# Two halves of a weighted sum made one task in a planned attention kernel

## The chip, the cores and the metric

One core of a Trainium2 chip runs the kernel. The metric is the time of one execution on the device in microseconds (us). The engines are called by their short names where rows are quoted: PE is TensorE (PEld its weight loads), DVE is VectorE, ACT is ScalarE, POOL is GpSimd, SP issues most DMAs.

## The reference

A backbone of two layers works on 512 latent tokens and 256 context tokens of width 1024. Each layer mixes tokens with three groups of heads that read one projection, joins their normalised outputs through one output projection, and then applies a SwiGLU feed-forward block. Two of the groups are attentions, and the change lies in them:

```python
# A: 6 heads of neighbourhood attention; a latent token sees a 2-D window and all context tokens
p = jax.nn.softmax(s.astype(jnp.float32), axis=-1).astype(v.dtype)
out = jnp.einsum('bhqrc,brqchd->bqhd', p_loc, v_win) + jnp.einsum('bhql,blhd->bqhd', p_ctx, v_ctx)
# C: 6 query heads over 2 key heads, all latent and context keys
s = jnp.einsum('bqkgd,bskd->bkgqs', q, k) * scale
p = jax.nn.softmax(s.astype(jnp.float32), axis=-1).astype(v.dtype)
return jnp.einsum('bkgqs,bskd->bqkgd', p, v)
```

Context tokens attend to context alone, and only in the first layer, since the output holds latent tokens only.

## The kernel before, in words

The attention of a layer is cut into units: one head and one tile of 128 queries. A latent unit of group A has 4 chunks of 128 keys, one of group C has 6, a context unit has 2. Layer 0 has 36 units of each group, layer 1 has 24 of each (no context queries). A unit goes through these steps: `scores` (L1311, TensorE, into a bank of the ring of PSUM tiles; 5 or 6 of them with group A, 3 wide ones with group C), `row_min` (VectorE, L1323 or L1329), `exps` (ScalarE, L1335), `trans` (L1343, TensorE transposes the probabilities chunk by chunk in place), `copy_p` (ScalarE L344 or VectorE L1349, from the bank into the tile `pT`; the bank is then free).

Two units in a row make a pair. `pv` (L1365) forms their weighted sums: for each chunk one matmul of the values with the transposed probabilities for each of the two units, whose results go to the lower and the upper 64 partitions of one of two PSUM banks called `aux`. Then come `evac` (L1371, VectorE copies the sum into `oT`), `back` (L1376, TensorE transposes it into another part of the same bank) and `norm` (L1381, two VectorE instructions that scale the rows by the reciprocal sums; the bank `aux` is free after them). The two `aux` banks also serve the transposes of other steps: `half` (L1408) for the operands of group C and `turn` (L1502) for the merged outputs of the groups, which the output projection then reads (`mtmp`, `xh`, `xl`). The last tile's outputs are turned by a step of the following phase (L1811). Matmuls of the projections go through one helper (L702 to L704).

The order of the instructions is set by a planner (`Plan`, L186 to L235). Each step is a task with an engine, an estimated duration, a priority, the tasks that it depends on, and tokens that it takes and gives (banks, tiles). The planner goes through an estimated time, and whenever an engine is free it emits the task with the lowest priority value that may start. A task is emitted whole, and the order in which tasks are emitted is the order in each engine's queue. At L1480 and L1481 `pv` is two tasks of one half of the chunks each. Both depend on the copies of both units, the first takes the bank, the second gives the two `pT` tiles back, and other TensorE tasks of lower priority value may be emitted between them. The projection weights of the next phase are split into two parts by ScalarE and VectorE or GpSimd, into tiles whose memory the attention's scratch tiles held before.

## Time and profile before

| | |
|---|---|
| median of 3 runs | 1722.39 us (1721.97 to 1726.96) |
| profiled execution, by its span | 1724.7 us |
| instructions | 25956 |
| TensorE busy | 1640.9 us, 95% |
| VectorE busy | 1085.3 us, 63% |
| ScalarE busy | 570.8 us, 33% |
| GpSimd busy | 940.8 us, 55% |

The profile gives no other time of the profiled execution than its span, from the first to the last instruction. The attention phase of layer 0 lies between some 205 and 372 us, that of layer 1 between some 1185 and 1304 us. A row of stretches names a window of time, its length, and the busy time of PE, PEld, DVE, ACT and POOL with the number of instructions, then the granted clock of TensorE as a share of the full one, the busy share of the DMA engines and GB/s. A row of waits names who waited for whom, the total in us, how often, and the longest. A row of the timeline has the start, the time until the last instruction of the group ended, the engine, line and operation; matmuls are pipelined, so that their rows overlap, and the step from one start to the next tells what one costs. The trace has two records for each matmul of the weighted sums.

### The profile page before, as it was taken

The numbers are of one execution on the slowest core, as the hardware profiler recorded it, in microseconds if no ns is written. First come the engines' busy times: TensorE is split into PE (matmuls) and PEld (weight loads), VectorE is DVE, ScalarE is ACT, GpSimd is POOL, SyncE is SP. The second block draws the span as 40 slices with busy tenths as digits, with TensorE's granted clock in tenths as the row PEclk, the third lists the DMA queues.
The fourth block names the chain that finished last, engine by engine and source line by source line (L and its number), as shares of the span: only waits on it lengthen the run. The fifth ranks groups of instructions, "written<-read, shape, count | busy, mean of one in ns | idle before, by whom it ended". The sixth has DMA issues, their size and how long they took to land. (4 is left out here: it accounts for less than half of the span.)

```text
span 1724.7 us, 25956 instructions
## 1 busy us (share of the span) xinstructions
PE 1640.9 (95%) x10438; PEld 1411.3 (82%) x10438; DVE 1085.3 (63%) x1691; ACT 570.8 (33%) x995; POOL 940.8 (55%) x683
## 2 busy tenths in 40 slices
PE   7999889999899999999999998998999999999997
PEld 5998767899888787887778878986889888888886
DVE  7567778748678796887932288527856544433435
ACT  5322368735411111111111234226764422222211
POOL 1764574434536664666744448445434466765762
PEclk9999999999999999999999999999999999999999
DMA  9326353041244423334231122212104133222211
GB/s 350 90 84 207 115 190 115 2 160 32 97 146 142 139 98 128 123 115 142 98 123 52 70 83 88 74 57 75 39 25 171 50 136 121 98 98 98 98 50 49
DMA packets 40264, 182.41 MB, mean 106 GB/s; under 512 B 4480, under 2 KB 6400, under 8 KB 29136
## 3 DMA queue, kind: packets, MB, share of 16 engines
q1 hardware_dynamic: 38336, 176.75, 29.3%
q0 software_dynamic: 1664, 3.75, 0.9%
q8 instruction: 82, 1.34, 0.3%
q14 instruction: 38, 0.31, 0.1%
q10 hardware_dynamic: 144, 0.26, 0.0%
HBM read 176.51 MB, written 6.78 MB: 106 GB/s over the span
## 5 line engine op out<-in xcount | busy, mean ns | idle before, releaser
L2005 POOL TENSOR_TENSOR x<-x,ytmp 128x1024 f32<-128x1024 f32 x90 | 249.3, 2793 | 26.7 <-DVE ytmp L2004 26.7
L347 POOL TENSOR_TENSOR gl<-sg,gh 128x512 fp32r<-128x512 f32 (+1 forms) x58 | 96.3, 1661 | 281.6 <-DVE gh L688 281.6
L652 DVE SCALAR_TENSOR_TENSOR msum<-raw,cs,msum 128x1024 f32<-128x1024 f32 x112 | 204.5, 1861 | 21.2 <-DMA raw<-in_w_mod_dram 21.2
L1980 DVE TENSOR_TENSOR sg<-sg,ff_ps 128x512 f32<-128x512 f32 (+1 forms) x58 | 34.4, 593 | 265.1 <-PE ff_ps L704 264.9
L2004 DVE TENSOR_TENSOR ytmp<-y_ps,g 128x512 f32<-128x512 f32 x180 | 119.0, 684 | 51.1 <-PE y_ps L704 51.0
L1979 ACT ACTIVATE sg<-ff_ps 128x512 f32<-128x512 f32 (+1 forms) x58 | 30.3, 523 | 293.6 <-PE ff_ps L704 293.6
L344 ACT ACTIVATE wc<-raw 128x1024 fp32r<-128x1024 f32 x52 | 52.7, 1053 | 160.7 <-PE y_ps L704 140.1
L702 PE MATMUL y_ps<-wc,gh 128*128 128x512 f32 x248 | 98.7, 398 | 0.0
L703 PE MATMUL y_ps<-wc,gh 128*128 128x512 f32 x248 | 98.0, 395 | 0.0
L704 PE MATMUL y_ps<-wc,gl 128*128 128x512 f32 x248 | 97.9, 395 | 0.0
L344 ACT ACTIVATE wa<-raw 128x1024 fp32r<-128x1024 f32 x60 | 62.2, 1056 | 105.0 <-PE ff_ps L703 43.4
L704 PE MATMUL ff_ps<-xh,wb 128*128 128x512 f32 x240 | 93.4, 389 | 0.0
L702 PE MATMUL ff_ps<-xh,wb 128*128 128x512 f32 x240 | 93.4, 389 | 0.0
L703 PE MATMUL ff_ps<-xl,wb 128*128 128x512 f32 x240 | 93.4, 389 | 0.0
L347 POOL TENSOR_TENSOR wb<-raw,wb 128x1024 fp32r<-128x1024 f32 x25 | 65.9, 2636 | 49.1 <-ACT wb L344 48.9
L347 POOL TENSOR_TENSOR wa<-raw,wa 128x1024 fp32r<-128x1024 f32 x29 | 78.0, 2689 | 20.2 <-ACT wa L344 20.1
L702 PE MATMUL ff_ps<-xh,wa 128*128 128x512 f32 x224 | 87.3, 390 | 0.0
L703 PE MATMUL ff_ps<-xl,wa 128*128 128x512 f32 x224 | 87.3, 390 | 0.0
L704 PE MATMUL ff_ps<-xh,wa 128*128 128x512 f32 x224 | 87.2, 389 | 0.0
L344 ACT ACTIVATE wb<-raw 128x1024 fp32r<-128x1024 f32 x54 | 55.4, 1056 | 88.1 <-DMA raw<-in_w_ffn_in_dram 39.8
L347 POOL TENSOR_TENSOR Kl<-kT,Kh 64x768 fp32r<-64x768 f32 x24 | 49.0, 2042 | 64.9 <-ACT Kh L344 61.6
L1343 PE MATMUL ring<-ident,p 128*128 128x128 f32 x528 | 75.1, 279 | 1.9 <-ACT p L1335 1.6
(527 smaller groups left out, 5421.4 us busy)
## 6 DMA issues: line engine op xcount, KB each, us to landing
raw<-in_w_ffn_in_dram SPq DMA_DIRECT2D x44, 1024.0 KB, 5.0
raw<-in_w_mod_dram SPq DMA_DIRECT2D x40, 1024.0 KB, 5.2
raw<-in_w_ffn_out_dram SPq DMA_DIRECT2D x22, 1024.0 KB, 5.0
raw<-in_w_in_dram SPq DMA_DIRECT2D x18, 1024.0 KB, 4.9
wm<-in_w_mod_dram SPq DMA_DIRECT2D x8, 1024.0 KB, 9.8
raw<-in_w_o_dram SPq DMA_DIRECT2D x8, 1024.0 KB, 5.1
tbz<-in_mask_dram SPq DMA_DIRECT2D x12, 384.0 KB, 3.4
x<-in_x_dram SPq DMA_DIRECT2D x8, 512.0 KB, 6.5
```

Of the source, the lines that this page charges most:

```text
L344: nc.scalar.activation(out=o, in_=i, func=AF.Copy, scale=scale)
L347: e.tensor_tensor(out=o, in0=a, in1=b, op=ALU.subtract)
L652: nc.vector.scalar_tensor_tensor(out=o, in0=w[:, i, :], scalar=c, in1=o, op0=ALU.mult, op1=ALU.add)
L702: nc.tensor.matmul(o, lhsT=lh, rhs=rh, start=(i == 0), stop=False)
L703: nc.tensor.matmul(o, lhsT=lh, rhs=rl, start=False, stop=False)
L704: nc.tensor.matmul(o, lhsT=ll, rhs=rh, start=False, stop=(i == n - 1))
L1343: nc.tensor.transpose(un.S[:, c:c + P], un.pt[:, j * P:(j + 1) * P], ident)
L1979: nc.scalar.activation(out=sg, in_=ab[0], func=AF.Silu)
L1980: nc.vector.tensor_tensor(out=sg, in0=sg, in1=ab[1], op=ALU.mult)
L2004: nc.vector.tensor_tensor(out=tmp[:, sl], in0=o, in1=G[1 if t >= NL else 0][:, sl], op=ALU.mult)
L2005: nc.gpsimd.tensor_tensor(out=x[:, t, :], in0=x[:, t, :], in1=tmp, op=ALU.add)
```

## The change

The two tasks of `pv` become one, with twice the estimated duration, the priority of the first half, the dependences of both, and both sets of tokens. The matmuls and their order inside a pair stay. The rest of the diff drops texts in quotes and comments, which moves line numbers by two or three (L1365 becomes L1363, L1376 L1374, L1408 L1406, L1502 L1499, L1811 L1808).

```diff
-        def pv(m, part):
-            """Outputs of two units, transposed, in the two halves of the partitions."""
+        def pv(m):
+
             pair = units[2 * m:2 * m + 2]
             u0 = pair[0]
-            if part == 0:
-                u0.o = aux.pop(0)
-            h = u0.nch // 2
-            for i in range(part * h, part * h + h):
+            u0.o = aux.pop(0)
+            for i in range(u0.nch):
                 for d, un in enumerate(pair):
                     nc.tensor.matmul(u0.o[d * HD:(d + 1) * HD, 0:P], lhsT=un.vs[i], rhs=un.pT[:, i, :], start=(i == 0), stop=(i == u0.nch - 1))
...
             h = {2: 0.27, 4: 0.54, 6: 0.8}[un.nch]
             c0, c1 = cpy_of[i - 1], cpy_of[i]
-            a_ = pn.op(PE, h, call(pv, m, 0), (c0[0], c1[0]), i + 1.7, take=("aux",), kind="pv " + un.kind)
-            b_ = pn.op(PE, h, call(pv, m, 1), (a_, c0[-1], c1[-1]), i + 1.8, give=("pT", "pT"), kind="pv " + un.kind)
+            b_ = pn.op(PE, 2 * h, call(pv, m), (*c0, *c1), i + 1.7, take=("aux",), give=("pT", "pT"), kind="pv " + un.kind)
```

Since the planner's inputs change, its order changes in both attention phases, and with it the order on the other engines. Three places on TensorE follow; a row names the line, the operation, what is written and read, the size and a count.

The first place is in the grouped-query units of layer 1, where the score matmuls of one unit (`ring` from `Kh`, `Kl` and `Q`) stand among the weighted sums. Before:

```order
L1365 MATMUL aux_10623<-pT,vc 64x128 x6
L1311 MATMUL ring_11271<-Kh,Q 128x512
L1311 MATMUL ring_11271<-Kl,Q 128x512
L1311 MATMUL ring_11271<-Kh,Q 128x256
L1311 MATMUL ring_11271<-Kl,Q 128x256
L1365 MATMUL aux_10623<-pT,vc 64x128 x6
L1502 MATMUL aux_10624<-ident,qT 128x128 x4
```

With the change:

```order
L1311 MATMUL ring_11295<-Kh,Q 128x512
L1311 MATMUL ring_11295<-Kl,Q 128x512
L1311 MATMUL ring_11295<-Kh,Q 128x256
L1311 MATMUL ring_11295<-Kl,Q 128x256
L1363 MATMUL aux_10623<-pT,vc 64x128 x12
L1374 MATMUL aux_10624<-ident,oT 128x128
```

The four score matmuls no longer stand between two runs of six; the twelve of a pair are one run. Over both phases the runs of weighted sums between other work number 91 before (56 in layer 0, 35 in layer 1) and 55 now (33 and 22).

The second place is the end of the attention of layer 1: the last weighted sums, the first two blocks of the output projection (24 matmuls each, of which the first rows are shown), and the transposes of the third tile's outputs, `qk`. Before:

```order
L1376 MATMUL aux_10623<-ident,oT 128x128
L1365 MATMUL aux_10624<-pT,vc 64x128 x6
L702 MATMUL ring_11273<-wa,xh 128x256
...
L1376 MATMUL aux_10624<-ident,oT 128x128
L1502 MATMUL aux_10623<-ident,qk 128x128 x3
L702 MATMUL ring_11273<-wa,xh 128x256
```

With the change:

```order
L1363 MATMUL aux_10623<-pT,vc 64x128 x12
L1374 MATMUL aux_10624<-ident,oT 128x128
L702 MATMUL ring_11294<-wa,xh 128x256
...
L1374 MATMUL aux_10623<-ident,oT 128x128
L702 MATMUL ring_11294<-wa,xh 128x256
...
L1499 MATMUL aux_10624<-ident,qk 128x128 x3
L702 MATMUL ring_11293<-wa,xh 128x256
```

The transposes of `qk` stood ahead of the second block and now stand behind it, right ahead of the third. The transposes of the last tile (L1811, now L1808) stood behind the third block, and now stand four blocks of `wb`, `wc` and `cb` later and more.

The third place is in the neighbourhood units of layer 1, around the transposes of the first operands of group C (`qn`). Before:

```order
L1365 MATMUL aux_10624<-pT,va 64x128 x4
L1343 MATMUL ring_10632<-ident,p 128x128 x4
L1343 MATMUL ring_10633<-ident,p 128x128 x4
L1376 MATMUL aux_10624<-ident,oT 128x128
L1408 MATMUL aux_10623<-identr,qn 128x128 x3
L1343 MATMUL ring_10628<-ident,p 128x128 x4
```

With the change:

```order
L1363 MATMUL aux_10624<-pT,va 64x128 x8
L1343 MATMUL ring_10633<-ident,p 128x128 x4
L1343 MATMUL ring_10628<-ident,p 128x128 x4
L1406 MATMUL aux_10623<-identr,qn 128x128 x3
L1374 MATMUL aux_10624<-ident,oT 128x128
L1363 MATMUL aux_10624<-pT,va 64x128 x8
```

A transpose back and the next weighted sum in the same bank now follow each other with nothing between. Layer 0 has one more such place; before there is none.

## The prediction

> **What bounds the kernel now.** I read the profile's head first, then a table of stretches that cuts out both attention phases, then TensorE's own waits in them, and last the timeline of TensorE around the changed matmuls.
>
> ```profile
> span 1724.7 us, 25956 instructions
> PE 1640.9 (95%) x10438; PEld 1411.3 (82%) x10438; DVE 1085.3 (63%) x1691; ACT 570.8 (33%) x995; POOL 940.8 (55%) x683
> ```
>
> TensorE is busy for 1640.9 of 1724.7 us. A change of its own work pays where it is busy without a gap, so the average over the program is not enough. The stretches, with columns for busy time of TensorE, its weight loads, VectorE, ScalarE and GpSimd, then the granted clock and DMA:
>
> ```profile
> 205.40:270.00 64.60, 58.12 (x507) 43.07 (x504) 50.61 (x136) 44.55 (x114) 37.65 (x23) 0.95 0.57 193
> 270.00:350.00 80.00, 79.11 (x742) 65.21 (x736) 59.98 (x148) 61.62 (x147) 37.99 (x53) 1.00 0.11 38
> 350.00:372.00 22.00, 22.00 (x203) 20.85 (x202) 9.57 (x16) 11.06 (x25) 11.35 (x14) 1.00 0.44 164
> 1185.00:1227.00 42.00, 36.57 (x361) 30.70 (x362) 37.99 (x101) 32.16 (x71) 30.01 (x19) 1.00 0.21 69
> 1227.00:1286.00 59.00, 58.35 (x569) 49.45 (x568) 43.47 (x95) 41.59 (x88) 23.18 (x32) 1.00 0.03 10
> 1286.00:1304.50 18.50, 16.65 (x128) 16.45 (x127) 7.05 (x10) 9.66 (x16) 7.26 (x9) 0.91 0.56 196
> ```
>
> The first three rows are layer 0: neighbourhood units, grouped-query units, their end. The last three are the same of layer 1. In the grouped-query stretches TensorE misses 0.9 of 80 us, nothing of 22 and 0.65 of 59 us, with VectorE at 75% and 74%: time taken off TensorE there should come out at the end. In the neighbourhood stretches it misses 6.5 of 64.6 us and 5.4 of 42 us, and in layer 1 VectorE is busy for 38.0 of the 42: there only part of it will pay. TensorE's waits (total, times, longest), layer 0 in the first two rows, layer 1 in the others:
>
> ```profile
> PE aux L1376 <- DVE oT L1371: 3.1, 2, 1.6
> PE aux L1365 <- DVE qT L1381: 2.3, 1, 2.3
> ...
> PE aux L1376 <- DVE oT L1371: 4.2, 3, 2.0
> PE ring L1811 <- POOL qk L1806: 1.9, 1, 1.9
> PE aux L1365 <- DVE qT L1381: 1.0, 1, 1.0
> ```
>
> These rows name the changed matmuls' neighbours: the transpose back (L1376) waits for the evacuation of a weighted sum (7.3 us in all), and a weighted sum (L1365) for a bank that the norms before it have to free (3.3 us).
>
> **The change, part by part.** Removed is the cut of each pair's weighted sum into two tasks. The matmuls stay: the orders of both kernels hold 528 at this line. Both halves already depended on the same two copies, so no half could start earlier than the whole can. What the cut cost is seen in the timeline (start, duration, then the instruction; the trace has two records to each of these matmuls):
>
> ```profile
> 310.34 0.28 PE L1311 MATMUL ring<-Kh,Q 128*128 128x256 f32 x1
> 310.45 0.28 PE L1311 MATMUL ring<-Kl,Q 128*128 128x256 f32 x1
> 310.66 0.44 PE L1365 MATMUL aux<-pT,vc 128*64 128x128 f32 x4
> 311.03 0.39 PE L1311 MATMUL ring<-Kh,Q 128*128 128x256 f32 x1
> 311.25 0.28 PE L1311 MATMUL ring<-Kl,Q 128*128 128x256 f32 x1
> 311.46 1.53 PE L1365 MATMUL aux<-pT,vc 128*64 128x128 f32 x24
> 312.92 0.33 PE L1376 MATMUL aux<-ident,oT 128*128 128x128 f32 x1
> 313.09 0.82 PE L1343 MATMUL ring<-ident,p 128*128 128x128 f32 x6
> 313.74 0.27 PE L1376 MATMUL aux<-ident,oT 128*128 128x128 f32 x1
> 313.85 1.04 PE L1343 MATMUL ring<-ident,p 128*128 128x128 f32 x8
> ...
> 314.94 0.60 PE L1502 MATMUL aux<-ident,qT 128*128 128x128 f32 x4
> 315.30 0.36 PE L1311 MATMUL ring<-Kh,Q 128*128 128x256 f32 x1
> 315.50 0.28 PE L1311 MATMUL ring<-Kl,Q 128*128 128x256 f32 x1
> ```
>
> Read start to start. A score matmul of 256 columns takes 0.11 (310.34 to 310.45) but 0.21 when a weighted sum follows (310.45 to 310.66): entering costs 0.10. Four records take 0.37 (310.66 to 311.03) and 24 take 1.46 (311.46 to 312.92): 1.09/20 = 0.0545 each, hence a fixed 0.37 - 4 x 0.0545 = 0.15 per run of them. The first score behind takes 0.22 in place of 0.11 (311.03 to 311.25): leaving costs 0.11. Leaving towards transposes costs less: the transpose behind the 24 takes 0.17, the next such one 0.11 (313.74 to 313.85), so 0.06. Nothing of this waits for data; no releaser stands at these rows. One run of weighted sums between other work therefore costs 0.10 + 0.15 + 0.06 = 0.31 us between transposes and 0.36 between scores. I take 0.31.
>
> [...]
>
> How often the cut costs it follows from the order: runs of weighted sums between other TensorE work fall from 91 to 55, 36 fewer. By stage: layer 0 neighbourhood 23 to 16, grouped-query 33 to 17; layer 1 14 to 11 and 21 to 11. That is 36 x 0.31 = 11.2 us of TensorE time, 26 x 0.31 = 8.1 of it in the grouped-query stretches that have no gaps, 10 x 0.31 = 3.1 in the neighbourhood stretches.
>
> Against it stand four terms, since the planner now places everything in both phases anew.
>
> Scores behind transposes: 45 such places become 53. The first score behind transposes takes 0.20 (315.30 to 315.50) in place of 0.11, so 8 x 0.09 = 0.7 us.
>
> Neighbourhood stretches: 3.1 us is at stake, and with 6.5 and 5.4 us of gaps present between nothing and all of it pays. I take half: 1.5 lost. The middle is as good as any since VectorE has slack in layer 0 (50.6 of 64.6) and little in layer 1.
>
> New short waits: work of one pair now stands closer to the next step. In two places the order has a transpose back and the next weighted sum in the same bank with nothing between, which no place of before has. There TensorE must wait for the two norms that free the bank:
>
> ```profile
> L1381 DVE TENSOR_SCALAR qT<-aux,rsm x60: 264/275/285, 217.0 to 1229.1; 128x64 f32<-128x64 f32 x60
> ```
>
> 0.27 for the transpose and 2 x 0.24 to 0.28 for the norms, with the handing over some 0.9 us, twice. The other direction exists too: a bank is now taken once and not held while other work runs between two halves, which works on the 3.3 us of bank waits above. From below I allow 3.3 us of gain (all of them vanish), from above 5 us of loss (half of the 10.6 us of waits at L1376 and L1365 once more). I take a loss of 2.0, the two known places and little else.
>
> The end of layer 1's attention. The order shows the transposes of the third tile's outputs (L1502) moved behind the second early block of the output projection. Rows of before, with the last weighted sum first:
>
> ```profile
> 1284.85 0.88 PE L1365 MATMUL aux<-pT,vc 128*64 128x128 f32 x12
> ...
> 1288.75 0.49 PE L1502 MATMUL aux<-ident,qk 128*128 128x128 f32 x3
> 1289.41 0.88 ACT L344 ACTIVATE mtmp<-aux,gout 128x128 f32<-128x128 f32 x3 [3.45 <-PE aux L1502]
> 1290.37 0.83 POOL L1525 TENSOR_TENSOR xh<-mtmp,zero 128x384 fp32r<-128x384 f32 x1 [2.60 <-ACT mtmp L344]
> 1291.28 1.02 POOL L347 TENSOR_TENSOR xl<-mtmp,xh 128x384 fp32r<-128x384 f32 x1
> 1292.33 1.06 ACT L344 ACTIVATE wb<-raw 128x1024 fp32r<-128x1024 f32 x1 [0.52 <-POOL xl L347]
> ...
> 1296.84 0.55 PE L1811 MATMUL ring<-ident,qk 128*128 128x128 f32 x3 [1.85 <-POOL qk L1806]
> ```
>
> From the transposes (1288.75) to the end of `xl` (1292.30) is 3.55 us. Before, an early block of about 2.9 us (24 x 0.12) covers that; now the third block, which needs `xl`, stands right behind, so TensorE waits about 3.55 - 0.45 = 3.1 us. In return the transposes of the last tile (L1811) move behind four more blocks, and their wait of 1.85 goes: 3.1 - 1.85 = 1.3 us lost. Queued behind `xl` are also the two weight copies on ScalarE (`wb`) and their differences on VectorE; the first copy takes 1.06 us by its row, and with a second copy, the square that stands between them and the last difference they need about 3.8 us after it, and the third block with its 2.9 us and the first half of the next cover that. After its gap the trace shows a lower granted clock (the third number from the end of a stretch's row):
>
> ```profile
> 1296.00:1300.00 4.00, 3.16 (x20) 3.16 (x21) 3.97 (x5) 1.62 (x4) 0.79 (x1) 0.76 0.67 231
> 1300.00:1304.00 4.00, 4.00 (x30) 4.00 (x30) 0.06 (x1) 2.01 (x2) 0.70 (x1) 0.81 1.03 385
> ```
>
> 0.76 and 0.81 for 4 us each, 0.24 x 4 + 0.19 x 4 = 1.7 us. If the longer gap doubles that, the loss is 3.0. I take 2.0.
>
> [...]
>
> The end of layer 0's attention has more cover than before (one early block between the last sum and its transpose back, and the blocks behind are in the same order), and no gap today: nothing. Behind both phases the weights stream as they do now.
>
> Sum: 11.2 - 0.7 - 1.5 - 2.0 - 2.0 = 5.0 us. The profiled execution took 1724.7 by its span; the runs go from 1721.97 to 1726.96 with a median of 1722.39, so 1719.7 for the former and **1717.4** for the median.
>
> **The rivals.** *The waits go with the cut.* The fused sum holds banks shorter; the 3.3 us of bank waits go and no new ones come: 11.2 - 0.7 - 1.5 + 3.3 - 1.3 = 11.0, 1711.4. For it: those waits are named. Against: two new tight places.
>
> *TensorE's gain turns into waits.* Three banks circle through scores, minimum, exponential, transposes, copy; when TensorE is faster the circle may become the bound. Then the 8.1 us of the grouped-query stretches go at least half: 5.0 - 4.0 = 1.0, 1721.4. For it: ScalarE and VectorE at 77% and 75% are not far off. Against: 0.9 us of gaps in 80.
>
> *Slower: the long block delays the circle.* Place: the pairs of grouped-query units whose sum has 24 records. Price: the block lasts 1.46 where one half lasted 0.81 (316.84 to 317.65 below), so a transpose or score that becomes ready in it comes up to 0.65 us later.
>
> ```profile
> 316.84 0.88 PE L1365 MATMUL aux<-pT,vc 128*64 128x128 f32 x12 [0.36 <-ACT mtmp L344]
> 317.65 0.44 PE L1343 MATMUL ring<-ident,p 128*128 128x128 f32 x2
> ```
>
> There are 24 such pairs by the order (288 of the 312 grouped-query matmuls, 12 each). If all pay, 24 x 0.65 = 15.6: 1717.4 + 15.6 = 1733. It decides from 16 pairs on (16 x 0.65 = 10.4, past 1727.6). Against: a late engine only costs if TensorE has nothing else to do, and today it always has.
>
> *The change doesn't do what it says:* the 0.3 us is no price of the switch and is paid elsewhere. Then only the losses are left: 1722.4 + 0.7 + 2.0 + 2.0 = 1727.
>
> **How the numbers follow.** My forecast (1713.5 to 1721) has 0.45, the vanishing waits 0.20, the gain turned into waits 0.20, the long block 0.11, the last 0.04. A measurement of this kernel can tell about 0.3%, 5.2 us, from no change: 1717.2 to 1727.6. Half of my forecast's chance lies below that and all of the vanishing waits: faster 0.43. Slower is the long block and a little of the rest: 0.15. The same: 0.42. The range for 8 of 10 goes from 1709.5 to 1727.5: below it is most of 36 x 0.36 = 13 us, above it the last rival.
>
> **What would show it.** Right: TensorE's busy time falls by some 10 us and the two grouped-query stretches shorten by 5 and 3 us with gaps still under 2 us; runs of weighted sums with 16 and 24 records in the timeline; a wait of about 3 us for `xl` at the end of layer 1's attention. Wrong: gaps there of 5 us and more with the transposes of the probabilities waiting for ScalarE (the gain turned into waits); TensorE's busy time unchanged (the last rival); a neighbourhood stretch longer by several us.

## The result, and the profile after

The changed kernel takes 1733.08 us (median of 4 executions, 1731.56 to 1733.29). The kernel before takes 1723.64 us (median of 4, three of them those of the table above). The ratio is 1.0051, with a 95% interval of 1.0037 to 1.0065: slower by half a per cent, some 8.8 us, where 1717.4 us had been forecast. The medians of the kernel before move between 1723.6 and 1726.3 us from one chip session to the next, so experiments are compared by ratio, and stage by stage by their profiles, one execution for each kernel. One execution among the experiments, the profiled one of a first session, took 3202 us and is not used.

The head of the profile of the changed kernel, with span, instructions and busy time per engine:

```profile
span 1731.3 us, 25941 instructions
...
PE 1638.7 (95%) x10438; PEld 1415.1 (82%) x10438; DVE 1087.4 (63%) x1691; ACT 570.1 (33%) x995; POOL 942.6 (54%) x683
```

The span is 6.6 us longer (1731.3 - 1724.7), though TensorE is busy for 2.2 us less. The forecast wanted some 10 us less. The stretches of the prediction, in the changed kernel (layer 0's grouped-query stretch, then layer 1's neighbourhood and grouped-query stretch; columns as before):

```profile
270.00:350.00 80.00, 76.81 (x740) 65.10 (x740) 59.68 (x144) 62.19 (x151) 38.68 (x54) 1.00 0.06 21
...
1185.00:1227.00 42.00, 33.78 (x326) 29.22 (x325) 34.22 (x91) 30.40 (x66) 30.06 (x20) 0.92 0.21 69
1227.00:1286.00 59.00, 55.89 (x544) 49.05 (x542) 45.32 (x92) 40.68 (x84) 18.44 (x27) 1.00 0.03 10
```

TensorE's gaps (the length less its busy time) have grown from 0.9 to 3.2 us of the 80, from 5.4 to 8.2 of the 42, and from 0.65 to 3.1 of the 59.

Windows of fixed time hold different work in the two kernels, so from here on a stage is cut by events that both have: (1) from the last transposes of the values in layer 0 to the transposes of the last tile (the attention), (2) from there to the first product into the feed-forward's output banks, (3) in layer 1 from the last transposes of the values to the last transpose back of a weighted sum, (4) from there to that layer's first such product. The four rows of the kernel before:

```profile
205.40:369.90 164.50, 157.13 (x1424) 127.03 (x1422) 118.28 (x295) 116.35 (x281) 86.99 (x89) 0.98 0.32 111
369.90:510.30 140.40, 131.08 (x990) 125.96 (x989) 96.61 (x152) 50.48 (x81) 57.46 (x49) 0.99 0.29 104
1175.00:1288.60 113.60, 106.05 (x1024) 90.20 (x1023) 91.30 (x215) 82.89 (x179) 59.80 (x56) 1.00 0.14 49
1288.60:1394.20 105.60, 98.41 (x785) 96.68 (x784) 59.34 (x86) 47.70 (x74) 45.31 (x40) 0.97 0.34 120
```

And of the changed kernel:

```profile
206.10:368.80 162.70, 152.90 (x1424) 126.30 (x1423) 119.89 (x296) 115.29 (x281) 86.16 (x89) 0.99 0.34 117
368.80:510.40 141.60, 131.40 (x989) 126.19 (x988) 94.17 (x150) 50.63 (x81) 57.07 (x49) 0.99 0.27 96
1175.00:1292.80 117.80, 105.22 (x1025) 92.48 (x1024) 91.44 (x215) 82.99 (x179) 58.43 (x56) 0.97 0.14 47
1292.80:1400.80 108.00, 99.61 (x786) 98.14 (x785) 61.93 (x86) 47.70 (x74) 48.92 (x41) 0.95 0.33 117
```

The stages moved by -1.8, +1.2, +4.2 and +2.4 us: 6.0 of the 6.6 (the rest is 0.7 us ahead of the first). Layer 0 barely gains, layer 1 loses 6.6. Where the granted clock is 0.5, TensorE's work took nearly twice as long (16 records of a weighted sum 1.98 us at 1192.02 in the changed kernel, and 1.09 us at full clock at 1185.12). What is lost by this half clock is estimated as the length times one minus the granted clock, and taken out of the busy time; in rows of 5 us it comes to 3.4 and 1.7 us in the first stage (before, changed), 1.7 and 1.7 in the second, nothing and 3.4 in the third, 3.4 and 5.1 in the fourth. The third stage then reads: TensorE's own work at full clock falls by 106.05 - (105.22 - 3.4) = 4.2 us, its gaps grow from 7.55 to 12.58 us, 5.0 more, and 3.4 us go to the half clock: -4.2 + 5.0 + 3.4 = 4.2. What the change was to save is there, and is paid back twice.

The two costs hang together. TensorE's waits in the third stage of the changed kernel (total, times, longest; L1374 is the transpose back):

```profile
PE aux L1374 <- DVE oT L1369: 7.2, 4, 3.1
PE ring L1343 <- ACT p L1335: 2.2, 3, 1.5
PE ring L1311 <- ACT pT L344: 1.5, 2, 1.1
```

Before, the first was 4.2 us and the others 1.2 and 0.4. The longest wait in TensorE's timeline:

```profile
1185.12 1.09 PE L1363 MATMUL aux<-pT,va 128*64 128x128 f32 x16
1186.14 0.66 PE L1343 MATMUL ring<-ident,p 128*128 128x128 f32 x4
1189.91 0.48 PE L1374 MATMUL aux<-ident,oT 128*128 128x128 f32 x1 [3.11 <-DVE oT L1369]
```

And VectorE's at the same place:

```profile
1185.62 1.81 DVE L998 CAST Q<-qT 64x512 fp32r<-64x512 f32 x1
1187.47 2.18 DVE L347 TENSOR_TENSOR Q<-qT,Q 64x512 fp32r<-64x512 f32 x1
1189.58 0.28 DVE L1369 COPY oT<-aux 128x128 f32<-128x128 f32 x1
```

GpSimd in the same time, and last the same subtraction on VectorE in the kernel before:

```profile
1185.33 1.82 POOL L347 TENSOR_TENSOR tbz<-tbz,traw 128x768 f32<-128x768 f32 x1
1187.23 1.87 POOL L347 TENSOR_TENSOR Kl<-kT,Kh 64x768 fp32r<-64x768 f32 x1
...
1187.65 0.69 DVE L347 TENSOR_TENSOR Q<-qT,Q 64x512 fp32r<-64x512 f32 x1
```

The sum is complete at about 1186.2. Its copy to `oT` takes 0.28 us, but stands behind two steps for a later head's operands, which take 4.0 us together. The second of them takes 2.18 us beside a subtraction on GpSimd; in the kernel before it took 0.69 us at 1187.65, where GpSimd ran nothing (its trace has no instruction from 1187.18 to 1188.83). So an order may also cost by what it lets meet on VectorE and GpSimd; no run takes that apart. Behind the wait the clock is at half (third number from the end):

```profile
1185.00:1190.00 5.00, 1.89 (x23) 1.36 (x22) 4.90 (x6) 3.44 (x7) 4.76 (x4) 0.87 0.35 110
1190.00:1195.00 5.00, 5.00 (x30) 4.45 (x31) 2.76 (x9) 2.49 (x3) 4.08 (x3) 0.50 0.04 11
```

### The profile page after: what moved, and what is told of

It is laid out like the page before. It is cut to its first block, busy times and chain, and to the rows that moved or that the text cites. A ratio compares the mean times of both kernels' runs of the same rounds, so it can differ in the third digit from the quotient of the medians.

```text
span 1731.3 us, 25941 instructions
## 1 busy us (share of the span) xinstructions
PE 1638.7 (95%) x10438; PEld 1415.1 (82%) x10438; DVE 1087.4 (63%) x1691; ACT 570.1 (33%) x995; POOL 942.6 (54%) x683
```

## The experiments

The theory after the first comparison: a run of weighted sums does cost some tenths of a microsecond, and what outweighs it is that the planner lays out both phases anew. Its rivals: the long block itself delays other work; VectorE's load bounds layer 1; the half clock behind the waits is the price.

### Issued in one go, with the order kept

The plan keeps its two tasks, so that everything else stands where it stood. The first takes the bank, and the second issues all matmuls of the pair.

```diff
             if part == 0:
                 u0.o = aux.pop(0)
-            h = u0.nch // 2
-            for i in range(part * h, part * h + h):
+                return
+            for i in range(u0.nch):
```

> The planner sees the two halves of before, so every other task keeps the place that it had before; only the matmuls of both halves are issued together where the second half stood. Runs of weighted sums between other TensorE work fall from 91 to 55, as in the changed kernel. Theory 1 (fusing saves about 0.31 us per run, and the changed kernel is slower because the planner placed everything else anew): faster than before by 4 to 10 us, 1714 to 1720, with the waits of the transposes back near the 7.3 us of before. Rival (the longer block itself delays what stands behind it, or fusing makes TensorE wait): slower than before, as the changed kernel is, by 5 to 10 us, 1728 to 1734.

Measured: 1722.27 us, ratio 0.9986 (0.9974 to 0.9997). Stages 1 and 3:

```profile
205.90:364.40 158.50, 150.52 (x1425) 126.03 (x1424) 117.15 (x295) 115.82 (x281) 87.27 (x89) 0.99 0.33 115
...
1169.10:1285.50 116.40, 104.50 (x1025) 91.71 (x1024) 91.75 (x215) 82.86 (x179) 59.79 (x56) 0.99 0.14 47
```

Layer 0's attention gains 6.0 us and keeps its gaps (7.37 before, 7.98 now). Of the 6.6 us that TensorE is busy less, 1.7 is a stretch of half clock that did not occur (3.4 before, 1.7 now), so 4.9 us belong to the 24 runs that are gone there: 0.20 us each. Layer 1 loses 2.8 us with the same edit: its gaps grow from 7.55 to 11.9, and one stretch of 1.7 us of half clock comes in. TensorE's waits there for evacuations rise from 4.2 to 7.0 us, those for exponentials from 1.2 to 2.5. Stage 4 takes 105.6 us as before. Long blocks alone are therefore a gain in layer 0, and a loss in layer 1.

### The same products at the place of the first half

```diff
-            if part == 0:
-                u0.o = aux.pop(0)
-            h = u0.nch // 2
-            for i in range(part * h, part * h + h):
+            if part == 1:
+                return
+            u0.o = aux.pop(0)
+            for i in range(u0.nch):
```

> As order_kept, but the matmuls of both halves are issued where the first half stood, so that a weighted sum ends no later than before and its evacuation and its transpose back have as much cover as before or more. 53 runs. Theory 1 (the saving is about 0.3 us for each of 38 runs; order_kept lost 2.8 us of it in layer 1, where issuing late moved the sums towards their transposes back): faster than before by 5 to 10 us, 1714 to 1719, with layer 1's attention no longer than before. Rival (layer 1's neighbourhood stretch is bound by VectorE, whatever the place of the sums): 1718 to 1720, layer 1 level with before.

> The plan of the kernel before; all products of a pair are issued where the first half stood, with the copies of the probabilities that the second half needed as their condition. A second look at this kernel, for an undisturbed trace. Theory (TensorE has to wait at the early place for the last copies of the pair's probabilities): 1728 to 1731 us, and waits of TensorE on those copies at the head of the weighted sums that come to 5 us or more in all, against none of that kind when they are issued at the later place. Rival (loss in the support engines, nothing at the head of the sums): the sums' own waits stay under 2 us and the loss shows as waits of transposes and back transposes in layer 1.

Measured: 1730.49 us, ratio 1.0025 (1.001 to 1.004), and in the second session 1729.08 us, 1.0019 (1.0003 to 1.0035). Theory and rival of the first session, both at 1720 us or less, missed. Stages 1 and 3 of the second session:

```profile
204.20:368.80 164.60, 153.21 (x1424) 126.76 (x1423) 117.99 (x295) 116.19 (x281) 87.61 (x89) 0.98 0.32 111
1173.90:1290.60 116.70, 104.42 (x1024) 90.14 (x1023) 91.36 (x215) 82.91 (x179) 59.77 (x56) 1.00 0.14 47
```

TensorE is busy 3.9 us less in layer 0 (157.13 to 153.21, with as much half clock as before) and stands idle 4.0 us more (7.37 to 11.39). All of it turns into waits, and layer 0 is level with the kernel before. Layer 1's stage 3 takes 3.1 us more. The second session's theory fits the time, but its picture of the waits was wrong: TensorE waits at the head of the sums for banks and not for copies of probabilities (in layer 0 2.3 us, as before; in layer 1 3.4 us in place of 1.5), and the transpose back waits for its evacuation in five places of layer 0 in place of two. The rival is nearer. So in layer 0 the place of the long block decides, by 6.1 us (158.5 against 164.6), and not its length; in layer 1 both places lose about 3 us.

### The change in one layer alone

The one task of the change in one layer, the two tasks in the other. This is the kernel with the change in layer 0 (`pv` with part 2 issues all chunks); the other has `l == 1` there:

```diff
+            if l == 0:
+                b_ = pn.op(PE, 2 * h, call(pv, m, 2), (*c0, *c1), i + 1.7, take=("aux",), give=("pT", "pT"), ...)
+            else:
                 a_ = pn.op(PE, h, call(pv, m, 0), ...)
                 b_ = pn.op(PE, h, call(pv, m, 1), ...)
```

> The real change, in layer 0 alone; layer 1 is planned as before. Runs fall from 91 to 68. The two profiles show layer 0 of the changed kernel ahead by 1 to 4 us at the end of its attention and level at 499 us. Theory 1: no change, within 2 us of before. Rival that the saving of layer 0 comes through at the end: faster by 2 to 5 us. Rival that the loss is spread over both layers: slower by 3 us or more.

> The real change, in layer 1 alone. Runs fall from 91 to 78. Theory 1: the whole loss sits here, slower by 6 to 10 us, with the wait of about 3.1 us of a transpose back for its evacuation near 1190 us and a lower granted clock behind it. Rival (the loss needs both layers): slower by less than 4 us.

Measured: layer 0 alone 1726.23 us, 1.0007 (0.9997 to 1.0017); layer 1 alone 1732.67 us, 1.0054 (1.0038 to 1.0069). By the ratios layer 1's part makes the whole loss, and layer 0's nothing that is clear of the noise. By their profiles stage 1 takes 162.8 us with the change in layer 0 alone, 4.3 more than with the order kept; stages 3 and 4 take 226.3 us with the change in layer 1 alone, 7.1 more than before. The attention of the layer that was not touched moves by up to 2.0 us (164.5 to 163.2, and 219.2 to 217.2 for stages 3 and 4), which is about what one profile tells of a stage.

### A new plan without the change

Two halves as before; the estimates of a half are 0.01 us longer in one kernel and 0.01 us shorter in the other, so that the planner lays out the same tasks in another order. The first of them (the other has 0.26, 0.53 and 0.79):

```diff
-            h = {2: 0.27, 4: 0.54, 6: 0.8}[un.nch]
+            h = {2: 0.28, 4: 0.55, 6: 0.81}[un.nch]
```

> The two halves stay; only the planner's estimates of a half are 0.01 us longer (0.28, 0.55 and 0.81 in place of 0.27, 0.54 and 0.8), so that the plan comes out another way with the same matmuls and nearly the same number of runs (90). Theory 1, in the form that any new plan costs some us because the table of priorities fits one plan: slower by 2 to 10 us. Rival (a new plan is as good as the old on the mean, and only fusing makes it worse): within 2 us of before.

> Two halves, the planner's estimates of a half 0.01 us shorter than before (0.26, 0.53, 0.79). Theory (any new plan is worse than the one that the priorities were made for, by some us): slower than before by 3 to 15 us. Rival (the other control was an unlucky plan): within 3 us of before.

Measured: 1738.89 us, 1.0089 (1.0068 to 1.011), and 1728.93 us, 1.0015 (1.0002 to 1.0029). Stage 1 of the two:

```profile
205.70:377.70 172.00, 158.27 (x1425) 126.34 (x1423) 117.03 (x295) 116.75 (x281) 87.87 (x89) 0.99 0.33 117
```

```profile
204.80:372.20 167.40, 159.25 (x1424) 127.04 (x1423) 117.83 (x295) 116.36 (x281) 86.31 (x89) 0.98 0.32 109
```

TensorE does 90 and 94 runs of weighted sums, about as before, and layer 0's attention still grows by 7.5 and 2.9 us. A new order by itself costs 10.5 and 4.4 us of span (1735.2 and 1729.1 against 1724.7); by the ratios, over all executions, it is some 15 and 3 us.

The change with another estimate goes the same way:

```diff
-            h = {2: 0.27, 4: 0.54, 6: 0.8}[un.nch]
+            h = {2: 0.3, 4: 0.52, 6: 0.73}[un.nch]
```

> The changed kernel with the estimate of a fused sum near what the trace shows (0.6, 1.04 and 1.46 us in place of 0.54, 1.08 and 1.6), so a third plan with 56 runs. Theory (the time of a fused kernel is the saving of about 10 us plus whatever the plan costs): between 1718 and 1740, with TensorE's busy time and the number of runs as in the changed kernel. Rival (the changed kernel is slower because its estimates were wrong): faster than before, under 1719.

Measured: 1734.91 us, 1.005 (1.0029 to 1.007). Its layer 0 attention takes 157.9 us, as good as with the order kept; its layer 1 takes 231.6 us for stages 3 and 4 together, 12.4 over before. Of four new orders, two with the change and two without, none is faster than the old one and none gains in layer 1 (222.5 and 220.1 us for stages 3 and 4 in the two without the change), and layer 0's attention differs by 14 us between them (157.9 to 172.0).

### The gain under a second plan

To see whether the gain of layer 0 belongs to the one plan, the second replan was given the same treatment as the first experiment: its order kept, all matmuls at the second half's place (the two edits above together).

> The second replan without the change (the halves estimated 0.01 us shorter: 1728.9 us), its order kept, and all products of a pair issued where the second half stood. Theory one (issuing in one go saves by itself some 6 us in layer 0 and nothing in layer 1, whatever the plan; what a new plan costs comes on top): layer 0's attention falls from 167.4 to about 161.5 us, layer 1's stretch stays within 3 us of 220.1, and the kernel takes 1722 to 1726 us. Rival (the 6 us belong to the one plan): layer 0's attention falls by less than 3 us and the time is 1727 us or more.

Measured: 1726.7 us, 1.0005 (0.9994 to 1.0016), 0.0010 below its own plan, a little above the expected range. Stages 1 and 3:

```profile
205.80:367.80 162.00, 152.25 (x1425) 126.36 (x1424) 117.24 (x296) 115.93 (x281) 86.58 (x89) 0.99 0.33 113
1172.50:1289.00 116.50, 104.91 (x1025) 91.81 (x1024) 92.47 (x215) 83.32 (x179) 59.55 (x56) 0.99 0.14 48
```

Layer 0's attention falls by 5.4 us (167.4 to 162.0), layer 1's grows by 2.7 (113.8 to 116.5). With the first plan it was -6.0 and +2.8. In layer 0 the theory holds; in layer 1, where it expected nothing, the loss comes again. Issuing in one go saves 5 to 6 us in layer 0, and costs 3 in layer 1, in either plan; what the plan costs comes on top. The sum of the two is small: the ratios' intervals of this kernel and of its own plan overlap.

### VectorE in layer 1: its order, and its load

Two kernels ask whether VectorE is the cause there. The first is the changed kernel with the operand steps of a later head put behind the evacuation wherever a sum had already been issued (four places in layer 1); TensorE's order is the same. `pend` counts the pairs whose sum is issued and whose copy is not, and the steps in `later` are issued once it is zero, or ahead of the scores that read their results.

```diff
-            q_ = pn.op(DVE, 0.47, parts[1], prio=p0, take=("Q",), kind="qhi")
...
+            q_ = pn.op(DVE, 0.47, lambda f=parts[1]: behind_evac(f)(), prio=p0, take=("Q",), kind="qhi")
...
+        def behind_evac(fn):
+            def go():
+                if l == 1 and pend[0]:
+                    later.append(fn)
+                else:
+                    fn()
+            return go
```

> The changed kernel with TensorE's order as it is; on VectorE, in layer 1 alone, the operand copies of the next head (Q, Kh) that stood ahead of an evacuation whose sum is already issued stand behind it, at four places. Theory (the loss of layer 1's attention is the waits of the transposes back of 0.8, 3.1, 2.2 and 1.1 us for evacuations that queue behind those copies, and the lower clock that follows): those waits fall to under 1 us each and the time by 4 to 8 us against the changed kernel, 1725 to 1729. Rival (VectorE is the bound of this stretch, so its order doesn't matter): within 2 us of the changed kernel, 1731 to 1735.

Measured: 1732.71 us, 1.0042 (1.0029 to 1.0056). TensorE's waits in stage 3, and the stage:

```profile
PE ring L1345 <- ACT p L1337: 4.8, 5, 1.5
PE aux L1394 <- DVE oT L1386: 4.1, 2, 2.7
PE ring L1313 <- ACT pT L344: 1.5, 2, 1.1
PE ring L1313 <- DVE Q L347: 1.2, 1, 1.2
```

```profile
1175.00:1292.70 117.70, 104.52 (x1024) 91.63 (x1023) 93.50 (x215) 82.93 (x179) 58.01 (x56) 0.99 0.14 47
```

The waits for evacuations fall from 7.2 to 4.1 us, those for the exponentials rise from 2.2 to 4.8, the scores wait 1.2 for operands, and the stage takes 117.7 us in place of 117.8. The theory had every wait for an evacuation under 1 us (the longest is 2.7) and 4 to 8 us of gain; the rival's time came. The wait that was taken away at one step came back at the next.

The other is a pair: before and changed, both with less work on VectorE in layer 1's attention.

```diff
-            nc.vector.reciprocal(out=un.rs, in_=un.sm)
+            if l == 0:
+                nc.vector.reciprocal(out=un.rs, in_=un.sm)
...
-            for d, un in enumerate(units[2 * m:2 * m + 2]):
+            for d, un in enumerate(units[2 * m:2 * m + 2] if l == 0 else ()):
                 nc.vector.tensor_scalar(out=un.dst, ...)
```

> The kernel before with VectorE relieved in layer 1's attention: the two multiplications by the reciprocal row sum and the reciprocal itself are left out for each pair (the output is then not the reference's), some 17 us of VectorE's 96 us there; everything else, order and plan, is the same. It is the pair of the next run. Both theories: a little faster than the kernel before, 1716 to 1724 us, since TensorE's waits for the copies of weighted sums (4.2 us there) become shorter.

> The changed kernel with the same relief of VectorE in layer 1's attention. Theory one (in layer 1 VectorE has no room where the new order lets work meet on it, so TensorE's shorter work turns into waits for it, one of them long enough to lower the clock): with the relief the gap between changed and before in layer 1, from the end of the turned values to the first output product, falls from 6.6 us to 2 us or less, and the changed kernel is no slower than its pair. Theory two (the new order and the long blocks themselves, whatever VectorE's load): the gap stays at 5 us or more, and this kernel is 7 us or more behind its pair.

Measured: 1724.64 us, 0.9993 (0.9979 to 1.0007), and 1729.08 us, 1.0018 (1.0007 to 1.0029). Stage 3 of the two, before and changed:

```profile
1172.90:1285.10 112.20, 105.23 (x1024) 90.10 (x1023) 80.81 (x145) 82.66 (x179) 59.70 (x56) 1.00 0.15 49
```

```profile
1174.50:1289.70 115.20, 103.87 (x1024) 91.66 (x1023) 81.55 (x145) 82.71 (x179) 59.73 (x56) 0.99 0.15 48
```

VectorE is relieved of 10 us in this stage (some 17 were expected); the kernel before gains 1.4 us by it, the changed one 2.6. The gap in layer 1 falls from 6.6 to 4.0 us (217.8 to 221.8 for both stages). That is neither theory's number: 2 or less was expected if VectorE's load is the cause, 5 or more if not. TensorE's wait for evacuations stays 7.2 us. VectorE's load is a part of it at most; the waits point at the place of its steps in the queue, which moving them in the kernel above did not prove.

### TensorE kept at work in the waits

The changed kernel with transposes of the identity ahead of the four instructions that waited longest in and behind layer 1's attention. Their results are written over or not read.

```diff
         def back(m):
             un = units[2 * m]
+            for _ in range({1: 18, 3: 12}.get(m, 0) if l == 1 else 0):
+                nc.tensor.transpose(aux[0][:, 0:P], ident, ident)
             nc.tensor.transpose(un.o[:, P:2 * P], un.oT, ident)
...
                         for j in range(2):
+                            if k == 0 and j == 1 and l_ == 1 and sc == SC2:
+                                filled.append(t0)
+                                for _ in range(20 if len(filled) == 1 else 28):
+                                    nc.tensor.transpose(tp[:, 0, 1, :], ident, ident)
                             nc.tensor.transpose(tp[:, i, j, :], ats[j]["n"][:, k * P:(k + 1) * P], ident)
```

> The changed kernel with TensorE kept at work during four of its waits in and behind layer 1's attention: 18, 12, 20 and 28 transposes of the identity (0.107 us each, so 1.9, 1.3, 2.1 and 3.0 us) ahead of the instructions that waited 3.11, 2.16, 2.71 and 3.86 us for VectorE. Theory one (the waits cost most of their price by the half clock that follows them: from 1175 to 1400 us the changed kernel lost 8.5 us to half clock, five stretches of 1.7 us, the kernel before 3.4 us, two): two or three of the five stretches go, the stretch from the end of the turned values to the first output product falls from 225.8 to 221 us or less, and the kernel takes 1728 to 1730 us. Theory two (VectorE and ScalarE set the pace there, and a TensorE at full clock only waits longer): the half clock goes, the waits grow by as much, and the kernel takes 1732 to 1734 us.

Measured: 1727.5 us, 1.0001 (0.9989 to 1.0013); the changed kernel alone stood at 1.0051. Stages 3 and 4:

```profile
1175.00:1290.40 115.40, 106.20 (x1055) 93.51 (x1054) 92.16 (x215) 82.99 (x179) 58.56 (x56) 1.00 0.15 48
1290.40:1395.50 105.10, 100.40 (x833) 98.91 (x832) 62.80 (x86) 47.46 (x74) 49.21 (x41) 1.00 0.34 120
```

The granted clock is 1.00 in both stages, where it was 0.97 and 0.95, and they take 220.5 us in place of 225.8. With 78 matmuls more the kernel is 5.3 us shorter there. The first theory's numbers are met or bettered (all five stretches of half clock go, and the time is 0.5 us under its range): of the 6.6 us that layer 1 lost, 5.3 come back, and against the kernel before 1.3 us remain. No run fills the kernel before, which has 3.4 us of half clock in stage 4, so the half clock's part in the difference of the two is 5.3 us at most. Stage 2, which the edit doesn't touch, took 143.6 us here in place of 141.6, at a granted clock of 0.95 in place of 0.99, which is some 7 us lost to half clock (0.05 x 143.6) in place of 1.7: so much did a stage change between two profiles, and some 5 us more of half clock came with 2.0 us more of stage.

### Layer 0 alone with the order kept, and filled

The experiments point to a version: the edit of the first experiment in layer 0, nothing in layer 1.

```diff
             if part == 0:
                 u0.o = aux.pop(0)
+                if l == 0:
+                    return
             h = u0.nch // 2
-            for i in range(part * h, part * h + h):
+            for i in range(part * h * l, part * h + h):
```

> The plan of the kernel before, order and all; in layer 0 all products of a pair are issued where the second half stood, in layer 1 nothing is touched. Theory one (a run of weighted sums costs TensorE about 0.3 us, and in layer 0 that gain reaches the end of the span when the plan is not redone): layer 0's attention falls from 164.5 to about 158.5 us, as in the run that kept the order in both layers, the rest stays, and the kernel takes 1716 to 1719 us (6 to 7 us under the one before). Rival (the gain of layer 0 comes back as waits in layer 1, whose stages start earlier against the weights' transfers): layer 1's attention to the first output product grows by 2 us or more and the time is 1720 to 1723 us.

Measured: 1720.58 us, 0.9975 (0.9961 to 0.9988). Its span is 1716.5 us, 8.2 below the profile of before. Layer 0's attention takes 158.50 us again, layer 1's two stages 113.5 and 105.7 (113.6 and 105.6 before); 1.8 us of the 8.2 lie ahead of stage 1. The median is over the expected 1716 to 1719 us and in the rival's range, but layer 1 doesn't grow by the 2 us that the rival needs. The kernel before stood at 1725.78 us beside it; 0.25% of that is 4.3 us. It beats both kernels, though by less than the 0.3% that the prediction set as a bound.

The same kernel with TensorE kept at work in four waits, as above: 16 transposes ahead of the seventh transpose back in layer 0, 14 ahead of each of two tile transposes behind it, 14 ahead of the turn at the end of layer 1's attention.

> The kernel that issues the products of a pair in one go in layer 0 alone with the order kept (1720.6 us, span 1716.5), and TensorE kept at work in four waits after which its clock had halved for 3.4 us: 16 transposes of the identity (0.107 us each) ahead of the back transpose that waited 2.45 us in layer 0's attention, 14 each ahead of the two tile transposes that waited 2.13 and 2.06 us behind it, and 14 ahead of the turn that waited 1.85 us at the end of layer 1's attention. Theory one (half clock there lies on the path: 1.7 us a stretch): three or four stretches go, the span falls to 1710 to 1713 us and the kernel takes 1714 to 1717 us. Theory two (VectorE sets the pace at these places, TensorE only waits longer): the span stays within 1.5 us of 1716.5 and the time at 1719 to 1721 us.

Measured: 1720.38 us, 0.9965 (0.9951 to 0.9979), span 1716.3. Stages 1 and 2 of it:

```profile
203.40:360.50 157.10, 150.84 (x1441) 126.57 (x1440) 117.24 (x295) 115.98 (x281) 87.44 (x89) 1.00 0.34 116
360.50:502.40 141.90, 134.60 (x1017) 129.06 (x1016) 96.59 (x152) 50.52 (x81) 58.05 (x49) 0.99 0.28 102
```

Only three of the four waits had half clock behind them in the unfilled kernel: behind the one of 2.06 us its rows from 440 to 450 us show 1.00, while 3.4 us were lost from 422 to 430, by rows of one microsecond, behind the wait of 2.13 us and across one of 1.75. Half clock in the four stages falls from 8.5 to 3.4 us by rows of 5 us, and the span by 0.2. Stage 1 gains 1.4 us (158.5 to 157.1) and stage 2 gives it back (140.4 to 141.9). There, and at the end of layer 1, other waits grew; in the unfilled kernel these were 1.75 and 1.45 us:

```profile
424.25 0.36 PE L702 MATMUL aux<-xh,wb 128*128 128x256 f32 x1 [2.39 <-DVE htmp L1638]
...
1351.00 0.90 PE L1741 MATMUL aux<-ident,n 128*128 128x128 f32 x3 [2.97 <-DVE n L1716]
```

So here the second theory holds: VectorE sets the pace behind the attention, and a TensorE at full clock arrives earlier and waits. The reading that fits both filled kernels is that half clock has a price where TensorE is late afterwards, as in the changed kernel's layer 1, and none where it is early anyway.

## Why the prediction was wrong

The forecast of 1717.4 us and its range (1709.5 to 1727.5) both miss 1733.08. Over the four stages the forecast can be held against the rows of the two profiles in three parts. TensorE's work at full clock was to fall by 10.5 us (11.2 - 0.7) and falls by 6.9. Its gaps were to grow by 4.8 us (1.5 + 2.0 + 1.3) and grow by 9.5. The half clock was to cost 0.7 us more and costs 3.4 more. The forecast sum is 5.0 us less, the measured one 6.0 more: of the 11.0 us between them 4.7 are gaps, 3.6 work and 2.7 clock. The steps in turn:

**36 runs of weighted sums less, 0.31 us each: right in kind, a third too large.** With the order kept, layer 0's 24 runs less give 4.9 us, 0.20 each, and under the second plan 26 runs less (59 to 33) give 7.0 us of busy time, 1.7 of it half clock, so again 0.20. In layer 1, 12 runs less take 106.05 - (104.50 - 1.7) = 3.25 us off TensorE, 0.27 each. 36 runs are then some 8 us, and not 11.2; in the changed kernel itself the two attention stages lose 6.8 us of work. The price was read at one place of the timeline. No run tells what on TensorE the 0.20 to 0.27 us go to. The rival that the change doesn't do what it says falls.

**That time taken off TensorE where it has no gaps comes out at the end: right in layer 0 and wrong in layer 1.** Stretches without gaps were read as having room for more. They showed only that TensorE was the last to arrive, by an amount that no row tells. With the order kept, layer 1 turns 3.25 us of gain into 4.35 us of gaps. The rival "TensorE's gain turns into waits" had this, but saw it in the circle of the banks; the waits that rise most are those for the evacuations on VectorE.

**New short waits, 2.0 us: the step that failed.** It counted two places where the order shows nothing between a transpose back and the next sum. But the new plan moved VectorE's and ScalarE's steps too, and their queues were not read. TensorE's gaps grew by 2.4, 0.9, 5.0 and 1.2 us in the four stages, 9.5 in all, twice the 4.8 of all terms together. Much of it sits at the transposes back, a row that the prediction shows: in stage 3 they wait 7.2 us for evacuations in place of 4.2, in stage 1 5.4 us (the row below) in place of 3.1. The two replans show that a new order can do this without the change: with two halves as before it costs 4.4 and 10.5 us of span. In layer 1 the order is not all: with the order kept, issuing in one go alone loses 2.8 of the 6.6 us.

```profile
PE aux L1374 <- DVE oT L1369: 5.4, 4, 2.4
```

**The end of layer 1's attention, 2.0 us: the size was near, the mechanism was not.** The 2.0 was an estimate between the 1.3 of the waits and the 3.0 with a second 1.7 us of lower clock. The forecast wait of 3.1 us for `xl` is not there: the third block does stand right behind the transposes, but 15 of its 24 matmuls run ahead of the first that waits (1296.02 to 1297.77). The waits there are 0.24 and 0.58 us, and 0.88 for `wb` behind them. Stage 4 is 2.4 us longer by later waits: two tile transposes wait 2.71 and 3.86 us for the norm on VectorE (0.92 and 1.44 before), and one more stretch of half clock follows. For the first of the two the norm itself is late: it takes 2.82 us, while GpSimd subtracts a weight piece, and its neighbour without that takes 0.80.

```profile
1299.37 0.39 PE L704 MATMUL ring<-wa,xl 128*128 128x256 f32 x1 [0.58 <-POOL xl L347]
...
1332.73 0.80 DVE L1706 TENSOR_SCALAR n<-x,cst 128x1024 f32<-128x1024 f32 x1
...
1335.05 2.34 POOL L347 TENSOR_TENSOR wb<-raw,wb 128x1024 fp32r<-128x1024 f32 x1
1335.12 2.82 DVE L1706 TENSOR_SCALAR n<-x,cst 128x1024 f32<-128x1024 f32 x1 [0.45 <-POOL cst L1643]
...
1337.99 0.55 PE L1725 MATMUL aux<-ident,n 128*128 128x128 f32 x3 [2.71 <-DVE n L1706]
```

**The clock: the missing term.** The forecast gave it 0.7 us at one place. Layer 1 has 8.5 us of half clock in the changed kernel and 3.4 before, and filling four waits gave 5.3 us back, the largest single part of the loss that a run takes away. In layer 1 of the two profiles it begins during or behind waits of TensorE (3.11, 2.71 and 3.86 us in the changed kernel, and 0.58 and 0.88 near 1301; 1.85 us before, and 0.45 to 1.24 near 1344), so it is read here as a part of their price and not as a cause of its own.

**Layer 0's end, nothing:** stage 2 took 1.2 us more, which is no more than one profile tells of a stage.

**Scores behind transposes (0.7) and half of the neighbourhood gain (1.5)** were not measured apart.

**The rival on the slow side** named 1733 us, which is what came, by a mechanism that the runs speak against: 24 long blocks that each delay the circle. The same blocks gain 6.0 us in layer 0 with the order kept. In layer 1 they lose 2.8, far from the 15.6 that the rival needs; there a delay by the long block is not ruled out as a part. That the number fits is chance.

What stays open: why issuing in one go loses some 3 us in layer 1 at either place and in either plan, and which of VectorE's and ScalarE's steps in layer 1 would have to move so that TensorE's gain is kept. Moving the operand steps shifted the waits, lighter norms took 2.6 us off the gap, and neither removed the loss.

## What to carry to other kernels

When an edit lets a list scheduler lay out a phase anew, price the new order apart from the edit: build the edit with the old order kept, and the old code under a slightly different estimate. Here the edit moved one layer by -6 us and the other by +3, and a new order alone cost 4.4 and 10.5 us of span. A stretch where TensorE has no gaps tells that it is last, not by how much, so read on the other engines' queues what stands ahead of the step that it will wait for, and ask for each long wait whether the clock falls behind it (here it fell behind one of 1.85 us, and not behind one of 2.39) and whether TensorE is late there.

## What the runs showed of the hardware that was not expected

Half clock came in pieces of one size. In the kernel with layer 0 alone and the order kept, the turn of the last tile in layer 1 ended a wait of 1.85 us at 1288.65; one row per microsecond from there:

```profile
1289.00:1290.00 1.00, 1.00 (x9) 1.00 (x8) 1.00 (x2) 0.76 (x3) 0.00 (x0) 0.82 0.53 131
1290.00:1291.00 1.00, 1.00 (x7) 1.00 (x6) 1.00 (x2) 0.12 (x1) 0.00 (x0) 0.50 0.94 385
1291.00:1292.00 1.00, 1.00 (x7) 1.00 (x7) 0.84 (x2) 0.00 (x0) 0.00 (x0) 0.50 1.03 434
1292.00:1293.00 1.00, 1.00 (x6) 1.00 (x6) 0.00 (x0) 0.03 (x1) 0.00 (x0) 0.50 0.92 377
1293.00:1294.00 1.00, 1.00 (x11) 1.00 (x10) 0.00 (x0) 1.00 (x2) 0.00 (x0) 0.97 1.04 426
```

0.18 + 3 x 0.50 + 0.03 = 1.71 us are lost, so 3.4 us at half clock. In the profiles read by rows of 5 us (before, changed, and this kernel without and with the filled waits) the loss in stage 1, in stage 2, and in stages 3 and 4 together was a multiple of 1.7 us each time (none to five). The length of the wait did not decide alone: half clock followed 1.85 us here, while 1.95 us at the transpose back at 1185.88 in the kernel before, and 2.39 us at 424.25 in the filled kernel, were followed by full clock.
